# A feed-forward down projection with the block product as the outermost loop, and its weight sums made earlier

## Chip, cores and metric

The kernel runs on one core of a Trainium2 chip. The metric is device time in microseconds (us) of that core, from the first to the last instruction, lower being better. Engines are named as in the profile: PE is TensorE (matmuls), PEld its weight loads, DVE is VectorE, ACT is ScalarE, POOL is GpSimd, SP is SyncE, which here only issues transfers.

## What is computed

One layer of an encoder with D = 1024 channels, L = 2048 positions and a feed-forward width of 4096, all in float32. Cut to what matters here:

```python
h = h + mixed @ w_out                                    # Hyena and mLSTM groups
h = h + cross_attention(rms_norm(h), rms_norm(mem), ...) # 4 heads, 256 memory tokens
h = h + square(relu(rms_norm(h) @ ff_w1)) @ ff_w2        # (2048,1024)@(1024,4096), (2048,4096)@(4096,1024)
return rms_norm(h, final_norm_g)
```

The change concerns the last line of the layer: the second product, here called the down phase (`ff_w2`, W2), and the places in attention and in the first product (the up phase, `ff_w1`) beside which sums of W2 blocks are made.

## The kernel before

**Stages.** The Hyena and mLSTM parts fill the first 1640 us or so, woven into the first chunks of `attention`. `attention` goes through four chunks of 512 positions; in each it makes the output projection (eight column tiles `ct`), the attention scores and values, and the attention output (eight more column tiles). Then `ffn` runs the up phase and the down phase.

**Order.** The tile framework gives every engine its own queue in an order planned from estimated costs: an instruction is put as early as its inputs and its buffers allow, earlier lines first among those that are ready. On the chip each queue then runs in that order, and an instruction that waits holds up those behind it on its engine. Buffers come from rings: a tag with `bufs=4` has four buffers, given out in program order; the next user of a buffer waits until all users of the one before are done. A pool that is opened after another has closed may use its memory.

**Precision.** Every float32 operand is split into a high and a low half (`halves`: ScalarE casts the high half, another engine subtracts it to get the low one), and every product is three matmuls (`mm3`): high x high, high x low, low x high.

**Seven products instead of eight.** Both feed-forward matrix products use the Winograd form of Strassen's scheme: of a 2 x 2 x 2 block product only seven block products are made, of sums of blocks; sums of the seven give the four result blocks. The products are numbered 1 to 7. For the up phase the positions' blocks (x) are summed by `sums_x`, on POOL: four blocks are loaded, four sums made and stored in the scratch tensor `xs`; the sums of W1's blocks are made on POOL in `load_w1` and `ffn_w1`. The four sums of the activated blocks (c11, c12, c21, c22, tag `q`, seven buffers) are made on POOL at product 3 of each group (`t`, four buffers) and stored in the scratch tensor `hc`.

**Where sums of x are made.** `attention` pops one entry of the list `sums` at every odd column tile: 20 empty ones, then four `sums_x` for the first half of the positions (tag `sm`, four buffers). `ffn` makes the other four at product 4 of groups 3, 5, 7 and 9 of the first half (`tp` = 0), in the same four `t` buffers as the sums of c.

**The up phase** goes through 16 groups `g` of 256 hidden channels for each half `tp` of the positions, and in each through the seven products (`ORDER_UP`): 224 steps of 12 matmuls.

**The down phase** sums over 32 blocks of 128 hidden channels, which are 16 pairs. The pairs are cut into four quarters `o` of four. The loop is `prods = [(o, i) for o in range(4) for i in ORDER_DOWN]`: for each quarter the seven products, for each product both position halves `tp`, and for each of these four steps `k`, each of 12 matmuls into four banks; again 224 steps.
- `load_w` loads three blocks of W2 per pair (`w`, in the pool `wring` that is also used for W1 and is open to the end), `sums_w` and `fetch_a` make their sums, on DVE for the first quarter and on POOL for the others, and `fetch_a` splits the operand into `ah`, `al` (four buffers each). The split is by DVE for the first six products and by POOL after that.
- `fetch_b` loads an activation block three steps ahead and splits it into `bh`, `bl` (six buffers each). Every block that is split at once passes through the ring `wr` (six buffers).
- After every four steps the four banks go to a tile `acc[i, tp]`: ScalarE copies 24 of them, DVE adds the other 200 to what is there. In the last quarter the seven `acc` tiles of each half are added to each other, on DVE and POOL.
- `residual` loads 32 blocks of h2 and scales them on POOL into `acc` tiles, in steps 4 to 35.
- `turned` transposes result blocks on TensorE, `finish` normalises and stores them.

Of the kernel before, what the change touches and what calls it, by code (L numbers as in the profile page):

```python
# [133 lines left out]
class Prog:  # L134
# [1165 lines left out]

    def attention(self, es):
# [24 lines left out]
        sums = [None] * 20 + list(range(4))  # L1326
# [39 lines left out]
        for c in range(4):  # L1366
# [19 lines left out]
            for ct in range(8):  # L1386
                yield 5.2
                if ct % 2 == 0:
                    w = next(wst)
                else:  # L1390
                    k = sums.pop(0) if sums else None
                    if k is not None:
                        self.sums_x(A, k, "sm")
# [91 lines left out]
            for ct in range(8):  # L1485
                yield 5.2
                if ct % 2 == 0:
                    w = next(wst) if ct else w
                else:
                    k = sums.pop(0) if sums else None  # L1490
                    if k is not None:
                        self.sums_x(A, k, "sm")
# [37 lines left out]
    def halves(self, src, tags, bufs, eng):  # L1530
        hi, lo = (self.R.tile([128, 512], F32R, tag=n, name=n, bufs=bufs) for n in tags)
        self.nc.scalar.copy(hi, src)  # L1532
        eng.tensor_tensor(lo, src, hi.bitcast(F32), ALU.subtract)  # L1533
        return hi, lo

    def ffn_open(self, es):
        self.R = es.enter_context(self.tc.tile_pool(name="ring", bufs=1, side="right"))
        self.xt = {}
        self.W, self.WD = {}, {}
# [67 lines left out]
    def ffn(self):  # L1607
# [5 lines left out]
        self.C = self.ctx.enter_context(tc.tile_pool(name="wring", bufs=1))  # L1613
        prods = [(o, i) for o in range(4) for i in self.ORDER_DOWN]
        down = [(n, tp, k) for n in range(len(prods)) for tp in range(2) for k in range(4)]
        aq, bq = {}, {}

        def fetch_a(n, k):
            o, i = prods[n]
            w = self.blocks_of(2, 4 * o + k)  # L1620
            eng = nc.vector if n < 6 else nc.gpsimd
            if i in (6, 7, 5):
                if i == 6:
                    eng.tensor_tensor(self.WD[k, 0], self.WD[k, 2], self.WD[k, 0], ALU.subtract)
                src = self.WD[k, {6: 0, 7: 1, 5: 2}[i]]
            elif i == 1:
                src = self.WD[k, 0]
            else:
                src = self.raw(w[i == 4][1])
                if i == 3:  # L1630
                    eng.tensor_tensor(src, src, self.WD[k, 0], ALU.subtract)
            aq[n, k] = self.halves(src, ("ah", "al"), 4, eng)

        def load_w(o, k):
            w = self.blocks_of(2, 4 * o + k)
            for j, src in enumerate((w[0][0], w[1][0], w[1][1])):
                t = self.WD[k, j] = self.wtile()
                nc.sync.dma_start(out=t, in_=src)

        def sums_w(k, op=nc.gpsimd.tensor_tensor):  # L1640
            op(self.WD[k, 2], self.WD[k, 1], self.WD[k, 2], ALU.add)
            op(self.WD[k, 1], self.WD[k, 0], self.WD[k, 1], ALU.subtract)

        def fetch_b(s, eng=nc.vector):
            n, tp, k = down[s]
            o, i = prods[n]
            bq[s] = self.halves(self.raw(hc[tp, i - 1, 4 * o + k]), ("bh", "bl"), 6, eng)

        with tc.tile_pool(name="up", bufs=1) as U:
# [23 lines left out]
            for n, (tp, g, i) in enumerate(steps):  # L1673
# [7 lines left out]
                if n + 9 >= len(steps) and n + 5 < len(steps):  # L1681
                    load_w(0, n + 9 - len(steps))
# [4 lines left out]
                if i == 4 and xsum and g % 2 and 2 < g < 13:  # L1687
                    self.sums_x(U, xsum.pop(0), "t")
# [34 lines left out]
        with tc.tile_pool(name="down", bufs=1) as B:  # L1723
            acc, ms = {}, []
# [6 lines left out]
            for i in (1, 6, 7, 4, 5, 3, 2):  # L1731
                for tp in range(2):
                    acc[i, tp] = B.tile([128, 4, 512], F32, tag="acc", name="acc", bufs=14)
# [3 lines left out]
            def residual(i, tp, k):  # L1737
# [222 lines left out]
```

## Time and profile before

| | |
|---|---|
| Median of three runs | 3217.77 us (3217.51 to 3219.89) |
| The profiled execution's own time | 3216.99 us |
| Its span, first to last instruction | 3215.3 us |
| Mean granted TensorE clock | 0.981 |
| Busy share of PE, DVE, ACT, POOL | 95%, 63%, 47%, 37% |
| Moved by DMA | 617.87 MB, 192 GB/s on average |

How to read the profile: every row of a timeline has a start and a duration in us, the engine (with a q for a transfer that its queue issues), the line of the kernel, the operation, the tiles it writes and reads, and in brackets how long the engine had stood idle and what ended that. Rows of groups have the count, the busy time, the mean duration in ns, and the idle time before them. Most DMAs of the stages treated here are of 256 KB. Matmuls overlap, so it is the distance of their starts that counts, not their durations.

### The profile page before, as it was taken

To read this page: it belongs to the slowest core of one execution; us is meant where nothing else is said; L and a number is where in the kernel's file an instruction comes from. 1 tells how busy PE (TensorE), PEld (TensorE's weight loads), DVE (VectorE), ACT (ScalarE), POOL (GpSimd) and SP (SyncE) were. 2 spreads that over 40 slices of the span, in tenths; PEclk is the share of its full clock that TensorE was granted. 3 is DMA by queue.
4 is the path that set the end of the run, shared out by engine and by line. 5 is a ranking of instruction groups with operands and counts; after the bars stand their busy time and mean duration, and the time that the engine had idled before them with its cause. 6 is when DMAs were issued, how large, how long until landed. Compare 5 with 4: busy or idle time off the path is not lost.

```text
span 3215.3 us, 43642 instructions
## 1 busy us (share of the span) xinstructions
PE 3047.5 (95%) x14473; PEld 2394.2 (74%) x14473; DVE 2036.0 (63%) x3439; ACT 1500.1 (47%) x2873; POOL 1182.7 (37%) x818
## 2 busy tenths in 40 slices
PE   6999999999999976999999998999999999999998
PEld 4655566876668765878887886888788878888876
DVE  7775366345865755667775547556645676556595
ACT  5533366434764343454444445455555443333335
POOL 0122012100121334224151217776756483434483
PEclk9999999999999997999999999999999999999999
DMA  5564776686687989657484537665644474444434
GB/s 189 191 206 162 247 201 202 178 274 185 180 235 209 295 281 280 195 174 246 141 276 141 182 111 243 215 198 179 201 152 153 157 246 154 144 129 150 125 92 167
DMA packets 453817, 617.87 MB, mean 192 GB/s; under 512 B 39630, under 2 KB 251726, under 8 KB 452568
## 3 DMA queue, kind: packets, MB, share of 16 engines
q1 hardware_dynamic: 415412, 556.57, 55.2%
q10 hardware_dynamic: 38180, 58.51, 5.5%
q8 instruction: 115, 1.88, 0.2%
q14 instruction: 110, 0.90, 0.1%
HBM read 416.73 MB, written 198.21 MB: 191 GB/s over the span
## 4 chain that ended last, share of the span: by engine, by line
PE 71%; DMA 13%; DVE 8%; issue 3%; ACT 3%; POOL 1%; SPq 1%; ACTq 0%; DVEq 0%; POOLq 0%
PE mm L339 15%; PE mm L341 15%; PE mm L340 15%; PE hy L341 5%; PE hy L339 5%; PE hy L340 5%; PE hy L176 2%; DMA rw<-rows 2%; PE hy L875 1%; PE mm L844 1%; PE hy L917 1%; DVE wl L344 1%; DMA xt<-in_x_t_dram 1%; DVE bl L1533 1%; DMA va<-vd 1%
## 5 line engine op out<-in xcount | busy, mean ns | idle before, releaser
L344 DVE TENSOR_TENSOR wl<-wn,wh 128x512 fp32r<-128x512 f32 (+1 forms) x364 | 289.0, 829 | 125.5 <-ACT wh L344 124.9
L1533 DVE TENSOR_TENSOR bl<-wr,bh 128x512 fp32r<-128x512 f32 x213 | 241.1, 1138 | 126.8 <-ACT bh L1532 123.2
L1532 ACT CAST ah<-w 128x512 fp32r<-128x512 f32 x284 | 176.3, 622 | 300.1 <-PE hy L340 154.8
L344 ACT CAST wh<-wn 128x512 fp32r<-128x512 f32 (+1 forms) x364 | 207.9, 618 | 209.3 <-PE mm L341 47.8
L922 POOL TENSOR_TENSOR b<-b,a 128x512 f32<-128x512 f32 x64 | 87.7, 1370 | 581.4 <-ACT b L920 457.1
L339 PE MATMUL mm<-xh,wh 128*128 128x512 f32 x640 | 270.1, 423 | 4.5 <-ACT xh L499 2.3
L1533 DVE TENSOR_TENSOR al<-w,ah 128x512 fp32r<-128x512 f32 x236 | 222.0, 942 | 58.6 <-ACT ah L1532 58.6
L340 PE MATMUL mm<-xl,wh 128*128 128x512 f32 x640 | 256.7, 402 | 1.9 <-DVE xl L344 1.4
L341 PE MATMUL mm<-xh,wl 128*128 128x512 f32 x640 | 258.1, 404 | 0.0
L1532 ACT CAST bh<-wr 128x512 fp32r<-128x512 f32 x232 | 143.7, 621 | 240.0 <-PE mm L341 177.0
L341 PE MATMUL mm<-bh,al 128*128 128x512 f32 x576 | 225.4, 394 | 8.0 <-DVE al L1533 4.7
L339 PE MATMUL mm<-bh,ah 128*128 128x512 f32 x576 | 226.6, 393 | 0.1
L340 PE MATMUL mm<-bl,ah 128*128 128x512 f32 x576 | 225.8, 392 | 0.0
L339 PE MATMUL mm<-act,wh 128*128 128x512 f32 x512 | 199.0, 394 | 4.2 <-ACT act L344 2.7
L340 PE MATMUL mm<-act,wh 128*128 128x512 f32 x512 | 201.2, 394 | 0.0
L341 PE MATMUL mm<-act,wl 128*128 128x512 f32 x512 | 200.0, 392 | 0.3 <-DVE wl L344 0.3
L1382 POOL TENSOR_TENSOR ssum<-ssum,sq 128x512 f32<-128x512 f32 x56 | 81.1, 1448 | 287.7 <-ACT sq L1381 287.7
L339 PE MATMUL hy<-bh,ah 128*128 128x512 f32 x448 | 175.2, 391 | 0.0
L340 PE MATMUL hy<-bl,ah 128*128 128x512 f32 x448 | 174.6, 390 | 0.0
L341 PE MATMUL hy<-bh,al 128*128 128x512 f32 x448 | 174.4, 390 | 0.0
L339 PEld LDWEIGHTS mm<-xh,wh 128*128 128x128 f32 x640 | 121.1, 189 | 65.4 <-issue 29.5
L339 PE MATMUL hy<-xh,ah 128*128 128x512 f32 x384 | 152.2, 397 | 8.9 <-ACT ah L1532 8.2
(367 smaller groups left out, 8439.4 us busy)
## 6 DMA issues: line engine op xcount, KB each, us to landing
wr<-hc SPq DMA_DIRECT2D x224, 256.0 KB
w<-in_ff_w_dram SPq DMA_DIRECT2D x176, 256.0 KB
hc<-t SPq DMA_DIRECT2D x128, 256.0 KB
wn<-in_w_in_dram SPq DMA_DIRECT2D x100, 256.0 KB
hc<-q SPq DMA_DIRECT2D x96, 256.0 KB
fs<-a SPq DMA_DIRECT2D x32, 512.0 KB
a<-fs SPq DMA_DIRECT2D x64, 256.0 KB
a<-zs SPq DMA_DIRECT2D x64, 256.0 KB
```

The costliest lines, as they stand in the source:

```text
L176: b = self.nc.tensor.matmul(*products[-1], start=True, stop=True)
L339: mm(ps, lh, rh, start=start, stop=False)
L340: mm(ps, lh, rl, start=False, stop=False)
L341: mm(ps, ll, rh, start=False, stop=stop)
L344: both = (self.nc.scalar.copy(hi, src), self.nc.vector.tensor_tensor(lo, src, hi.bitcast(F32), ALU.subtract))
L844: nc.tensor.matmul(pp, dm[:, m], t[:, m], start=True, stop=True)
L875: nc.tensor.matmul(pg, em[:, m], y, start=True, stop=True)
L917: nc.tensor.matmul(pp, dm[:, m], t[:, m], start=True, stop=True)
L922: nc.gpsimd.tensor_tensor(xt, xt, hi[:, m], ALU.mult)
L1382: nc.gpsimd.tensor_tensor(ssum, ssum, sq, ALU.add)
L1532: self.nc.scalar.copy(hi, src)
L1533: eng.tensor_tensor(lo, src, hi.bitcast(F32), ALU.subtract)
```

## The change

The product becomes the outermost loop of the down phase: `prods = ORDER_DOWN`, and for each product and each half of the positions 16 steps `k`, one for each pair. The four banks collect all 16 steps, so they are emptied 14 times and not 56 times. All 16 split blocks of a product are kept for both halves: the first four in `ah`, `al`, the other twelve in `dh`, `dl` in the pool `down`. `fetch_a` loads a block, or a ready sum of blocks, and splits it on DVE; for the first product blocks 4 to 15 are fetched four steps ahead, for the others at the step of the second half in which the buffer is last used. All activation splits go to DVE.

The sums of W2's blocks are made by a new method `sums_w`, on POOL, and stored in a scratch tensor `ws`: for pairs 0 and 1 ahead of the four `sums_x` of attention, for pairs 2 to 11 behind them, and for pairs 12 to 15 in the up phase at product 4 of groups 4, 6, 8 and 10. `load_w` and the sums in the down phase go. The pool `wring` now closes with the up phase's pool.

The results of the products are put together as they come (`close`): DVE adds a bank to a running sum `T[role, tp]` (product 1 is copied by ScalarE), which makes 56 additions on DVE from banks and 8 copies. The residuals are loaded, scaled and added on POOL, one per step, when the sum they go to is there (`jobs`). Transposes are made at every third step.

```diff
+    def sums_w(self, pool, g, tag):
+        op = self.nc.gpsimd.tensor_tensor
+        ws = self.dram("ws", (4, 16, 128, 512))
+        w = self.blocks_of(2, g)
+        t11, t12, t21, t22 = self.four(pool, [w[m][k] for m in range(2) for k in range(2)], tag)
+        op(t22, t21, t22, ALU.add)
+        op(t21, t11, t21, ALU.subtract)
+        op(t11, t22, t11, ALU.subtract)
+        op(t12, t12, t11, ALU.subtract)
+        for j, t in enumerate((t22, t11, t21, t12)):
+            self.nc.sync.dma_start(out=ws[j, g], in_=t)
...
-        sums = [None] * 20 + list(range(4))
+        sums = [None] * 16 + [partial(self.sums_w, A, g, "sm") for g in range(2)]
+        sums += [partial(self.sums_x, A, i, "sm") for i in range(4)] + [partial(self.sums_w, A, g, "sm") for g in range(2, 12)]
...
-        self.C = self.ctx.enter_context(tc.tile_pool(name="wring", bufs=1))
-        prods = [(o, i) for o in range(4) for i in self.ORDER_DOWN]
-        down = [(n, tp, k) for n in range(len(prods)) for tp in range(2) for k in range(4)]
+        prods = self.ORDER_DOWN
+        down = [(n, tp, k) for n in range(len(prods)) for tp in range(2) for k in range(16)]
+        ws = self.dram("ws", (4, 16, 128, 512))
...
+        def fetch_a(n, k, *own):
+            w = self.blocks_of(2, k)
+            src = {1: w[0][0], 2: w[0][1], 4: w[1][1], 5: ws[0, k], 6: ws[1, k], 7: ws[2, k], 3: ws[3, k]}[prods[n]]
+            aq[n, k] = self.halves(self.raw(src), *(own or (("ah", "al"), 4, nc.vector)))
...
+        with tc.tile_pool(name="wring", bufs=1) as self.C, tc.tile_pool(name="up", bufs=1) as U:
...
-                if n + 9 >= len(steps) and n + 5 < len(steps):
-                    load_w(0, n + 9 - len(steps))
...
-                if i == 4 and xsum and g % 2 and 2 < g < 13:
-                    self.sums_x(U, xsum.pop(0), "t")
+                if i == 4 and tp == 0 and 2 < g < 11:
+                    if g % 2:
+                        self.sums_x(U, xsum.pop(0), "t")
+                    else:
+                        self.sums_w(U, 10 + g // 2, "t")
...
+            def residual(tp, n, h, role, k):
+                own = role == "c22"
+                v = T[role, tp][:, k] if own else B.tile([128, 512], F32, tag="rs", name="rs", bufs=3)
                 nc.sync.dma_start(out=v, in_=h2[2 * tp + n, :, 4 * h + k])
                 nc.gpsimd.tensor_tensor(v, v, ms[2 * tp + n], ALU.mult)
+                dst = v if own else T[role, tp][:, k]
+                nc.gpsimd.tensor_tensor(dst, v, T["u3", tp][:, k] if own else dst, ALU.add)
...
+            def close(i, tp, bank, last):
+                def plus(dst, role):
+                    for m in range(4):
+                        d = V.tensor_tensor(dst[:, m], bank[m], T[role, tp][:, m], ALU.add)
...
+                def late(n, h, role):
+                    jobs.extend(partial(residual, tp, n, h, role, k) for k in range(4))
+                if i == 1:
+                    T["m1", tp] = block()
+                    for m in range(4):
+                        nc.scalar.copy(T["m1", tp][:, m], bank[m])
+                elif i == 6:
+                    T["u2", tp] = block()
+                    plus(T["u2", tp], "m1")
+                    late(0, 0, "m1")
+                elif i == 7:
+                    T["u3", tp] = block()
+                    plus(T["u3", tp], "u2")
+                    T["c22", tp] = block()
+                    late(1, 1, "c22")
+                else:
+                    role = {5: "c22", 3: "u2", 2: "m1", 4: "u3"}[i]
+                    plus(T[role, tp], role)
+                    if i == 5:
+                        plus(T["u2", tp], "u2")
+                        late(1, 0, "u2")
+                        late(0, 1, "u3")
+                    outs.extend(turned(tp, i in (5, 3), i in (5, 4), role))
             for s, (n, tp, k) in enumerate(down):
...
+                if s + 3 < len(down):
+                    fetch_b(s + 3)
+                if n == 0 and tp == 0 and k < 12:
+                    fetch_a(0, k + 4, ("dh", "dl"), 12, V, B)
+                if jobs:
+                    jobs.pop(0)()
...
-                    self.mm3(bank[m], ah[:, msl], al[:, msl], bh, bl, k == 0, k == 3)
+                    self.mm3(bank[m], ah[:, msl], al[:, msl], bh, bl, k == 0, k == 15)
                 if tp and n + 1 < len(prods):
-                    fetch_a(n + 1, k)
+                    fetch_a(n + 1, k, *((("dh", "dl"), 12, V, B) if k > 3 else ()))
+                if outs and k % 3 == 2:
                     outs.pop(0)("mm" if tp else "hy")
...
+                if k == 15:
+                    close(prods[n], tp, bank, s + 1 == len(down))
```

123 lines of the change are left out of this document (24 added, 99 removed).

## The prediction

> **What bounds the kernel now.** First the page: the span and the engines' shares.
> ```profile
> span 3215.3 us, 43642 instructions
> PE 3047.5 (95%) x14473; PEld 2394.2 (74%) x14473; DVE 2036.0 (63%) x3439; ACT 1500.1 (47%) x2873; POOL 1182.7 (37%) x818
> ```
> TensorE works 95% of the span. So an edit pays only where TensorE stands still, and costs only where it makes TensorE stand still. The busy time by stage says where that is (columns: window, length, busy time of PE, PEld, DVE, ACT, POOL with counts, granted clock, DMA share, GB/s).
> ```profile
> 1800.00:1930.00 130.00, 130.00 (x595) 108.11 (x594) 65.59 (x122) 53.82 (x110) 19.58 (x14) 1.00 0.32 107
> 1975.00:2135.00 160.00, 160.00 (x708) 132.48 (x707) 100.29 (x125) 86.36 (x145) 128.15 (x87) 1.00 0.66 215
> 2295.00:2560.00 265.00, 265.00 (x1171) 219.44 (x1170) 145.35 (x203) 136.14 (x222) 156.56 (x110) 1.00 0.49 162
> 2560.00:2660.00 100.00, 95.19 (x406) 77.77 (x406) 81.92 (x72) 45.06 (x81) 77.01 (x48) 0.97 0.67 224
> 2660.00:3110.00 450.00, 449.75 (x1984) 372.17 (x1984) 290.51 (x347) 144.09 (x245) 205.66 (x143) 1.00 0.43 132
> 3110.00:3198.00 88.00, 84.26 (x417) 68.76 (x415) 63.32 (x112) 48.38 (x109) 50.58 (x37) 0.98 0.42 138
> ```
> Undisturbed, one matmul takes 265.00/1171 = 0.226 us, so a step of the down phase (12 matmuls) takes 2.72 us, before and after the change: 224 steps either way, with 128 transposes either way. The down phase (2560 to 3198) is therefore already near its floor. What it loses is in the list of TensorE's waits for that stretch, and in the clock behind the two long ones.
> ```profile
> PE mm L341 <- DVE al L1533: 4.7, 1, 4.7
> PE mm L341 <- POOL al L1533: 3.3, 2, 3.0
> ```
> ```profile
> 2648.44 0.39 PE L340 MATMUL mm<-bl,ah 128*128 128x512 f32 x1
> 2653.54 0.79 PE L341 MATMUL mm<-bh,al 128*128 128x512 f32 x1 [4.71 <-DVE al L1533]
> 2654.13 0.63 PE L339 MATMUL mm<-bh,ah 128*128 128x512 f32 x1
> 2654.56 0.63 PE L340 MATMUL mm<-bl,ah 128*128 128x512 f32 x1
> ```
> ```profile
> 2653.00:2662.00 9.00, 8.46 (x25) 6.76 (x26) 7.66 (x9) 4.47 (x9) 4.12 (x3) 0.64 0.81 256
> 3117.00:3122.00 5.00, 4.80 (x15) 3.58 (x16) 5.00 (x5) 1.14 (x2) 5.00 (x4) 0.67 0.30 101
> ```
> After the first wait matmuls start 0.43 us apart (2654.13, 2654.56): the clock is 0.64 for 9 us, another 9 x 0.36 = 3.2 us. After the second, 5 x 0.33 = 1.7 us. The whole loss is 4.7 + 3.3 + 3.2 + 1.7 = 12.9 us. That is all the down phase has to give.
>
> **Start of the down phase: +1.4 us.** Twelve of the 16 blocks of the first product get buffers (`dh`, `dl`) in the pool that is opened when the up phase's pool has closed. Block 4 is needed at step 4.
> ```profile
> 2560.72 0.39 PE L339 MATMUL mm<-bh,ah 128*128 128x512 f32 x1
> 2572.06 0.39 PE L339 MATMUL hy<-bh,ah 128*128 128x512 f32 x1
> ```
> ```profile
> 2559.98 0.69 DVE L1641 TENSOR_TENSOR w<-w 128x512 f32<-128x512 f32 x1 [2.91 <-DMA w<-in_ff_w_dram]
> 2565.51 0.68 DVE L1663 TENSOR_TENSOR q<-mm,u 128x512 f32<-128x512 f32 x1
> 2567.60 1.29 POOL L1713 TENSOR_TENSOR t<-q 128x512 f32<-128x512 f32 x1 [16.71 <-ACT q L1665]
> 2572.25 1.74 POOL L1716 TENSOR_TENSOR t<-q,t 128x512 f32<-128x512 f32 x1
> 2574.01 0.32 SPq L1654 DMA_DIRECT2D hc<-t  x1
> 2576.69 1.75 SPq L1729 DMA_DIRECT2D on<-msd  x4
> 2577.10 2.05 ACT L1815 COPY acc<-mm 128x512 f32<-128x512 f32 x4 [6.94 <-DMA hc<-t]
> ```
> ```profile
> L1532 ACT CAST ah<-w 128x512 fp32r<-128x512 f32 x62 | 38.7, 624 | 91.0 <-PE hy L340 91.0
> ```
> The new pool's first uses (`on`, `acc`) come at 2576.7 to 2577.1, when the last store of the up phase (2574.01) has landed. If that stays, block 4 is cast (0.62) and split (0.69) by 2578.0, TensorE stands 5.9 us at step 4 (2572.06), and loses about 3 us more at the lower clock: 9 us. ScalarE would stand in the same wait, with the casts of activations behind it; those of the next steps are as early as now. But the store's chain starts with the last `q`, at 2565.51, although its bank was full when the down phase's first matmul started, by 2561: VectorE was held up by a W2 sum that waited 2.91 us for its load, and by other sums, all of which the change removes. With `q` at 2561.0 the store lands 4.5 us earlier, at 2572.2, and block 4 is ready at 2573.5: a wait of 1.4 us. Ends 0 and 9; I take the 1.4, since every operation in the way is one of those removed.
>
> **Down phase, steady part: -12.9 us.** Both waits are for a split of a W2 block (`al`), which a product needs four steps after the last one used its buffer, and behind which stand sums of blocks, late loads and POOL.
> ```profile
> L1533 DVE TENSOR_TENSOR bl<-wr,bh 128x512 fp32r<-128x512 f32 x203 | 230.1, 1139 | 122.4 <-ACT bh L1532 118.8 <-DMA wr<-hc 1.4 <-DMA wr<-in_ff_w_dram 1.2
> L1817 DVE TENSOR_TENSOR acc<-mm,acc 128x512 f32<-128x512 f32 x100 | 64.5, 682 | 38.3 <-PE mm L341 38.3
> L1817 DVE TENSOR_TENSOR acc<-hy,acc 128x512 f32<-128x512 f32 x100 | 64.2, 679 | 16.5 <-PE hy L341 16.4
> L1533 POOL TENSOR_TENSOR al<-w,ah 128x512 fp32r<-128x512 f32 x48 | 67.5, 1409 | 119.7 <-ACT ah L1532 119.7
> L1533 POOL TENSOR_TENSOR al<-wr,ah 128x512 fp32r<-128x512 f32 x40 | 54.7, 1371 | 100.0 <-ACT ah L1532 100.0
> ```
> After the change a block is split 16 steps (43 us) ahead, not four (11 us); the sums come ready from memory. VectorE gives up about 200 - 56 = 144 evictions at 0.68 us (98 us) and the 24 closing adds, and takes 88 splits over from POOL and 15 of the activations. A half with weight splits then needs two splits a step: 2 x 0.69 = 1.4 us (as the sum at 2559.98, with POOL idle) or 2 x 1.14 = 2.3 us (the mean here), under 2.72 either way. POOL keeps 32 residuals of two operations of 1.4 to 1.7 us, about 100 us, and no split, so nothing of it feeds TensorE quickly. Loads: 224 activations and 112 blocks, against 224 and 96 now, at a similar rate (132 GB/s). Six activation splits (`bh`, six buffers) still run ahead, 13 us; four or eight evictions in a row (2.7 or 5.4 us) fit inside; they are what is late next, if anything. I take the whole 12.9 us as gained; the other end is one new wait like that at 2653, 7.9 us. The closing chain keeps its four adds, 16 transposes and output writes: 0.
>
> [...]
>
> **Attention: +2 us.** Twelve sums of W2 blocks (four loads, four POOL operations, four stores each) use the four `sm` buffers in order, two ahead of the four sums of x and ten behind them.
> ```profile
> PE hy L1463 <- POOL ssum L1382: 4.0, 1, 4.0
> ```
> ```profile
> 1681.22 1.29 POOL L1293 TENSOR_TENSOR sm<-sm 128x512 f32<-128x512 f32 x1 [0.94 <-issue]
> 1696.65 1.26 POOL L1293 TENSOR_TENSOR sm<-sm 128x512 f32<-128x512 f32 x1 [3.49 <-DMA sm<-hg]
> 1697.87 1.26 POOL L1382 TENSOR_TENSOR ssum<-ssum,sq 128x512 f32<-128x512 f32 x1
> ```
> The sums now run as soon as their input is there, one per 15.4 us (1681.22 to 1696.65). The last sum of x started at 1696.65, so the tenth behind it starts near 1851 and ends near 1860, ahead of the up phase (1930); POOL has room (19.58 of 130 us) and so have the DMAs (107 GB/s, and 2 MB per 15.4 us are 136 more). What they can cost is seen in the rows: POOL stood 3.49 us for a load with a square sum queued behind it, and TensorE waited 4.0 us for that (about 6 with the lower clock). The next such point is the end of chunk 3's first half, in the middle of the added sums. SP's queue gets 8 more transfers per sum, and a store that waits for POOL holds up weight loads behind it; those have four buffers ahead. Ends 0 and 6; I take 2, a third, since sums would fill about half of POOL's time there and only one that waits for its load does harm.
>
> **Up phase: +2 us.** Four sums of W2 go beside groups 4, 6, 8 and 10; groups 3, 5, 7 and 9 have their sums of x already. All share four `t` buffers with the block sums of c, in program order.
> ```profile
> 2041.07 1.29 POOL L1713 TENSOR_TENSOR t<-q 128x512 f32<-128x512 f32 x1 [2.71 <-ACT q L1665]
> 2054.12 1.50 POOL L1293 TENSOR_TENSOR t<-t 128x512 f32<-128x512 f32 x1 [4.16 <-DMA t<-hg]
> 2057.50 1.30 POOL L1294 TENSOR_TENSOR t<-t 128x512 f32<-128x512 f32 x1 [0.64 <-POOL w L1582]
> 2063.88 1.29 POOL L1713 TENSOR_TENSOR t<-q 128x512 f32<-128x512 f32 x1
> 2079.15 1.29 POOL L1713 TENSOR_TENSOR t<-q 128x512 f32<-128x512 f32 x1 [3.10 <-ACT q L1665]
> ```
> Two groups take 2079.15 - 2041.07 = 38.08 us, 19.04 each. With a sum of x between, c's sums start 22.8 us after those of the group before (2041.07 to 2063.88), and the next group makes good the 3.8 us. After the change no group does until the tenth. A sum of W2 starts with the last-loaded blocks (2057.50, not 2054.12), so 22.8 to 26.2 us; by estimate 24.5. The lag after eight groups: 4 x 3.8 + 4 x 5.5 = 37 us. `q` has seven buffers, four per group, so the fourth of the next group waits once c's sums are about 19 - 1.3 = 17 us late (less the time of two activations); eight PSUM banks let TensorE go on for up to another group, 19 us, if the rest is queued well. So TensorE loses between 0 and 37 - 17 = 20 us. I take 2, from the row that is nearest: with lags of 3.8 us TensorE was busy 160.00 of 160.00 us. POOL would be busy 128 + 16 x 1.4 = 151 of 160 us.
>
> **Sum.** -12.9 + 1.4 + 2 + 2 = -7.5 us. The profiled execution took 3216.99 us, which makes 3209.5; the median of the runs is 0.8 us higher: 3210 us. About 0.2%, 6.4 us, is what a measurement of this kernel can tell from no change: faster is below 3211.3, slower above 3224.2.
>
> **Rivals.** *The ring of `t` buffers becomes the bound in the up phase* (slower). For it: the 37 us of lag, the DMAs at 0.66 share with 8.4 MB more in 160 us, 32 more transfers in SP's queue among W1's loads, and W1's sums behind POOL's waits for loads (the 4.16 us). Against: banks and `q` buffers. Price 20 us in place of 2: 3228 us. It decides from a loss of 16 us. Chance 0.31.
>
> *The new pool opens as late as now* (no change): 9 us at step 4 instead of 1.4: 3218 us. For it: 2576.69. Against: the sums that are gone. Chance 0.15.
>
> *The change doesn't do what it says*: the down phase waits elsewhere, since loads and splits still pass through six `wr` buffers and one queue in order; one wait like 2653's, +7.9: 3218 us. Against: two waits in 224 steps, both at W2 blocks. Chance 0.12.
>
> [...]
>
> **Numbers.** The forecast has 0.42: faster. The two rivals at 3218 make no change 0.27, the first slower 0.31. Below, all added costs at nothing give 3217.8 - 12.9 = 3204.9, and 2 us for a shorter close; above, the first rival with 6 us in attention in place of 2 gives 3232, and a slower clock behind its waits a little more. The likeliest case alone: 3203 to 3211.
>
> **What would show it.** In the down phase no wait of TensorE over 1 us after step 4, and POOL near 100 us in place of 333. At step 4, about 1 us of wait for `dl` (9 with the clock: second rival). In 1975 to 2215 TensorE full; a wait there for `al`, `ah` or a bank, with c's sums more than 16 us late, is the first rival. I am wrong altogether if the up phase starts later than now (the tenth sum of W2 still open at 1930), or if TensorE's pitch differs from 0.226 us.

## The result and the profile after

The changed kernel takes 3269.2 us (median of five runs, 3266.1 to 3275.4), the kernel before 3219.4 on the same chip: 1.0158 times as long, 95% interval 1.0143 to 1.0172. The forecast was 3210 with a range to 3233, so it was wrong: the kernel became 50 us slower. First the page and the busy time by stage of the changed kernel, then the same four stages in the kernel before (window, length, busy time of PE, PEld, DVE, ACT, POOL with counts, granted clock, DMA share, GB/s).

```profile
span 3267.4 us, 43690 instructions
PE 3069.9 (94%) x14473; PEld 2401.6 (74%) x14473; DVE 1928.0 (59%) x3358; ACT 1491.9 (46%) x2857; POOL 1038.8 (32%) x723
...
1240.00:1297.00 57.00, 28.51 (x166) 26.49 (x165) 31.09 (x87) 16.25 (x67) 29.17 (x23) 0.65 0.87 282
1711.00:1830.00 119.00, 105.56 (x464) 85.45 (x465) 64.60 (x108) 46.01 (x97) 52.86 (x39) 0.93 0.79 265
2090.00:2250.00 160.00, 144.90 (x605) 117.31 (x605) 74.65 (x101) 67.72 (x117) 118.08 (x84) 0.95 0.65 215
2614.00:3252.00 638.00, 636.08 (x2813) 518.29 (x2812) 311.44 (x454) 229.09 (x414) 103.32 (x68) 1.00 0.51 161
```
```profile
1240.00:1285.00 45.00, 26.19 (x158) 24.85 (x159) 24.41 (x80) 15.30 (x64) 19.32 (x15) 0.66 0.83 256
1699.00:1798.00 99.00, 98.65 (x458) 81.28 (x459) 54.84 (x110) 46.22 (x98) 13.62 (x11) 0.98 0.55 183
2058.00:2218.00 160.00, 160.00 (x707) 132.48 (x707) 92.59 (x118) 84.81 (x139) 117.27 (x82) 1.00 0.56 183
2560.00:3198.00 638.00, 629.20 (x2804) 518.69 (x2803) 435.75 (x529) 237.53 (x434) 333.25 (x227) 0.99 0.46 147
```
The rows from 1240 on are the same work ahead of attention's chunk 0 in both kernels, and those from 1711 and 1699 the second half of chunk 2: both have become longer, and the DMA engines are fuller there. The rows from 2090 and 2058 lie 124 us into the up phase: there TensorE worked all of 160 us before and 145 after. In the down phase POOL is down from 333 to 103 us, as forecast, and TensorE is full, and yet the phase is no shorter. TensorE's waits in the changed kernel, for chunk 2's second half and chunk 3, the up phase and the down phase, and last the longest of the up phase in the kernel before:

```profile
PE hy L1356 <- DMA wn<-yh: 6.5, 2, 6.3
PE hy L1476 <- POOL ssum L1395: 4.0, 2, 3.7
PE hy L1356 <- DMA wn<-ym: 2.5, 1, 2.5
...
PE hy L339 <- ACT ah L1545: 21.0, 6, 4.7
PE hy L341 <- DVE al L1546: 4.5, 4, 2.7
...
PE mm L339 <- ACT dh L1545: 1.9, 1, 1.9
...
PE hy L339 <- ACT ah L1532: 8.2, 3, 4.6
```
The two waits of the down phase are gone; what is left is 1.9 us at step 4 (forecast 1.4). But 21.0 us of waits for `ah` stand in the up phase (8.2 in the kernel before) and 13.0 in attention's three rows (4.0 before). In the stretches that hold the long ones the granted clock was 0.93 and 0.95 (0.98 and 1.00 before).

The stages of every kernel below, from the first rows of their matmuls (start: first `act` matmul of chunk 0; attention: from there to the first `xh,ah` matmul of the up phase; up: from the first to the last of these; down: from there to the last `bh` row of L339; all us, each of one profiled execution; last the median, beside that of the kernel before measured with it):

| kernel | start | attention | up | down | median / before |
|---|---|---|---|---|---|
| before | 1285.3 | 648.5 | 626.2 | 636.5 | |
| after | 1296.7 | 669.2 | 648.3 | 636.2 | 3269.2 / 3219.4 |
| loop_alone | 1287.2 | 646.1 | 624.6 | 636.6 | 3217.6 / 3219.2 |
| sums_alone | 1301.8 | 669.4 | 650.3 | 636.2 | 3273.2 / 3219.2 |
| mid_sums | 1287.6 | 665.9 | 623.5 | 636.2 | 3232.8 / 3219.2 |
| dl_high | 1298.1 | 670.2 | 647.3 | 636.3 | 3269.5 / 3219.2 |
| loop_moved | 1292.3 | 649.0 | 624.5 | 625.1 | 3205.4 / 3224.5 |
| mid_staged | 1293.9 | 663.1 | 631.1 | 636.3 | 3237.2 / 3224.5 |
| staged | 1287.9 | 666.5 | 642.3 | 625.0 | 3240.9 / 3224.5 |
| mid_traffic | 1292.4 | 669.6 | 624.5 | 636.2 | 3239.4 / 3219.6 |
| late | 1290.0 | 654.5 | 636.6 | 626.6 | 3219.5 / 3219.6 |
| late2 | 1290.3 | 648.2 | 636.3 | 628.8 | 3217.3 / 3221.0 |

From before to after: +11.4 at the start, +20.7 in attention, +22.1 in the up phase, -0.3 in the down phase and -1.8 behind it make the 52.1 us by which the span grew. How far single executions scatter shows in kernels that have no sum of W2 in a stage: the start lies between 1285.3 and 1293.9, attention between 646.1 and 651.3, the up phase between 623.5 and 626.2 (without mid_staged, see below).

### The profile page after: what moved, and what is told of

The parts are those of the page before. It is cut to its first block, busy times and chain, and to the rows that moved or that the text cites. A ratio compares the mean times of both kernels' runs of the same rounds, so it can differ in the third digit from the quotient of the medians.

```text
span 3267.4 us, 43690 instructions
## 1 busy us (share of the span) xinstructions
PE 3069.9 (94%) x14473; PEld 2401.6 (74%) x14473; DVE 1928.0 (59%) x3358; ACT 1491.9 (46%) x2857; POOL 1038.8 (32%) x723
## 4 chain that ended last, share of the span: by engine, by line
PE 68%; DMA 15%; DVE 6%; issue 3%; POOL 3%; ACT 3%; SPq 1%; ACTq 0%; POOLq 0%; DVEq 0%
PE mm L339 14%; PE mm L340 14%; PE mm L341 14%; PE hy L341 5%; PE hy L339 5%; PE hy L340 5%; PE hy L176 3%; DMA hc<-t 2%; DVE wl L344 1%; PE hy L875 1%; PE mm L844 1%; PE hy L917 1%; DMA wn<-in_xa_wo_dram 1%; DMA rw<-rows 1%; DMA wn<-in_xa_wq_t_dram 1%
## 5 line engine op out<-in xcount | busy, mean ns | idle before, releaser
L1546 DVE TENSOR_TENSOR bl<-wr,bh 128x512 fp32r<-128x512 f32 x228 | 187.8, 826 | 203.7 <-ACT bh L1545 203.1
L1546 DVE TENSOR_TENSOR al<-w,ah 128x512 fp32r<-128x512 f32 x220 | 204.6, 931 | 121.8 <-ACT ah L1545 121.6
L339 PE MATMUL mm<-xh,wh 128*128 128x512 f32 x640 | 270.9, 424 | 5.4 <-ACT xh L499 3.2
L1545 ACT CAST ah<-w 128x512 fp32r<-128x512 f32 x220 | 135.3, 619 | 235.0 <-PE mm L340 103.8
L339 PE MATMUL mm<-act,wh 128*128 128x512 f32 x512 | 201.0, 398 | 9.0 <-ACT act L344 3.0
L339 PE MATMUL hy<-xh,ah 128*128 128x512 f32 x384 | 155.4, 405 | 21.8 <-ACT ah L1545 21.0
L339 PEld LDWEIGHTS mm<-xh,wh 128*128 128x128 f32 x640 | 121.6, 190 | 65.9 <-issue 29.2
L341 PE MATMUL hy<-xh,al 128*128 128x512 f32 x384 | 155.1, 404 | 4.5 <-DVE al L1546 4.5
L340 PEld LDWEIGHTS mm<-xl,wh 128*128 128x128 f32 x640 | 121.1, 189 | 50.9 <-issue 24.2
L340 PE MATMUL hy<-xl,ah 128*128 128x512 f32 x384 | 154.4, 402 | 1.8 <-POOL xl L1570 1.8
L339 PE MATMUL mm<-wh,xh 128*128 128x256 f32 (+1 forms) x512 | 152.3, 299 | 4.0 <-ACT st L202 3.3
L341 PEld LDWEIGHTS mm<-xh,wl 128*128 128x128 f32 x640 | 121.2, 189 | 41.3 <-issue 17.6
L339 PE MATMUL mm<-xh,ah 128*128 128x512 f32 x384 | 149.9, 390 | 0.0
L340 PE MATMUL mm<-xl,ah 128*128 128x512 f32 x384 | 149.8, 390 | 0.0
```

The source lines that it names most:

```text
L339: mm(ps, lh, rh, start=start, stop=False)
L340: mm(ps, lh, rl, start=False, stop=False)
L341: mm(ps, ll, rh, start=False, stop=stop)
```

## The experiments

**The loop alone, and the sums alone.** `loop_alone` has no `sums_w` call, and plain blocks where the loop reads sums:

```diff
-            src = {1: w[0][0], 2: w[0][1], 4: w[1][1], 5: ws[0, k], 6: ws[1, k], 7: ws[2, k], 3: ws[3, k]}[prods[n]]
+            src = {1: w[0][0], 2: w[0][1], 4: w[1][1], 5: w[0][0], 6: w[1][0], 7: w[1][1], 3: w[0][1]}[prods[n]]
```


> The new loop order without any sum of W2: products 5, 6, 7 and 3 read plain blocks of W2 of the same size in place of the sums, so the output leaves out the sums; loads, halves and matmuls of the down phase are the changed kernel's. Theory (the sums cost all of the loss, the loop alone is worth nothing because its matmuls are slower): the up phase starts at 1934 and lasts 627 as in the kernel before, the down phase lasts 636 as in the changed kernel, total 3217 to 3223, same. Rival 1 (the loop costs time by itself, through its later start or its larger set of halves): above 3235. Rival 2 (the slower matmuls come from the sums' traffic, not from the loop): the distance between two matmuls with dh or dl falls to 227 ns, the down phase to 625, total 3207 to 3211.

`sums_alone` is the kernel before with `sums_w` and its calls added, the result unused.

> The kernel before, with the sums of W2 made and stored at the changed kernel's places and used by nobody. Theory (the sums cost the loss, in three places that add up: 11 to 13 ahead of attention's first chunk, 19 to 21 in attention's chunk 2, 22 in the up phase): the up phase starts at 1966, lasts 648, the down phase lasts 636 as in the kernel before, total 3268 to 3276. Rival (the loss comes from both halves of the change together, since the loop's new buffers also shift the rest): under 3250.

Measured: loop_alone 0.9995 times the kernel before (0.9983 to 1.0007), sums_alone 1.0167 (1.0141 to 1.0193). The first `xh,ah` matmul of the up phase, in loop_alone and in sums_alone:

```profile
1933.31 0.50 PE L339 MATMUL hy<-xh,ah 128*128 128x512 f32 x1 [0.75 <-ACT xh L1568]
```
```profile
1971.16 0.50 PE L339 MATMUL hy<-xh,ah 128*128 128x512 f32 x1 [0.75 <-ACT xh L1569]
```
The halves of the change add up: the sums carry the whole loss, and the loop gains nothing, although its waits are gone. That leaves two questions: what ate the loop's gain, and what the sums cost where.

**What ate the gain: the place of `dh` and `dl`.** The changed kernel's matmuls were only slower with certain weights. Four rows of it: the first matmul of a half with `ah`, 48 later the first with `dh`, 144 later the first with `ah` of the next half, 48 later `dh` again.

```profile
2661.44 0.40 PE L339 MATMUL hy<-bh,ah 128*128 128x512 f32 x1
...
2672.38 0.40 PE L339 MATMUL hy<-bh,dh 128*128 128x512 f32 x1
...
2705.84 0.39 PE L339 MATMUL mm<-bh,ah 128*128 128x512 f32 x1
...
2716.74 0.40 PE L339 MATMUL mm<-bh,dh 128*128 128x512 f32 x1
```
With `ah` and `al`, 10.94/48 and 10.90/48 give 228 and 227 ns a matmul; with `dh` and `dl`, 33.46/144 is 232.4 ns, at a granted clock of 1.00 and with TensorE busy all of the time. The down phase has 2016 such matmuls: 2016 x 5.7 ns = 11.5 us, the gain. The first guess was the distance from `bh`: `dl` was put behind the ten `acc` blocks.

```diff
+            B.tile([128, 512], F32R, tag="dh", name="dh", bufs=12)
+            block()
```


> The changed kernel with the 12 buffers of dl placed behind the ten blocks of acc, at byte 125,024 to 149,600 of a partition, in place of 43,104 to 67,680; dh stays at 18,528. Nothing else differs. In the changed kernel a matmul with dh or dl comes 232.5 ns after the one before, with ah or al (byte 212,960 and up) 226.7 to 227. Theory 1 (the place of the stationary tile in the partition sets the pace, far from the moving tile bh at 188,384 being slow): the matmuls whose weight load falls on dl come down toward 227 to 230 ns, the rest stay at 232.5; the down phase is 2 to 4 shorter, total 3264 to 3268. Theory 2 (it isn't the place: the number of buffers, the pool or the program's length): all stay at 232 to 233, total 3269 within 2.

All rows stayed at 232.3 to 232.7 ns (232.4 in the changed kernel): theory 1 fell, and `dl` low or high in the partition, at byte 43,104 or 125,024, made no difference. But at both places the tiles begin 96 bytes beyond a multiple of 512, since the 128-byte tile `ss` is allocated ahead of them, while `ah` and `bh` begin 480 beyond one. `loop_moved` moves one line:

```diff
-            ss = B.tile([128, 4, 2, 4], F32, name="ss")
...
+            for n in ("dh", "dl"):
+                B.tile([128, 512], F32R, tag=n, name=n, bufs=12)
+            ss = B.tile([128, 4, 2, 4], F32, name="ss")
             V = nc.vector
```


> loop_alone (the new order, plain blocks in place of the sums, so the output leaves the sums out) with the small tile ss (128 bytes of a partition) placed behind dh and dl in place of ahead of them: dh then begins at byte 18,400 and dl at 42,976 of a partition, both 480 beyond a multiple of 512, as bh (188,384) and ah (212,960) do; in loop_alone, the changed kernel and dl_high they begin 96 beyond one. Theory (the place of the stationary tile modulo some power of two up to 512 sets the pace): every row with dh or dl falls from 232.5 ns to 226.7 to 228, the down phase from 636.5 to 624 to 627, total 3204 to 3210 beside 3219 before, faster. Rival (the pace comes from something else: the left end of the partition, the number of buffers): rows stay at 232 to 233, total 3216 to 3222.

The 144 matmuls from the first with `dh` to the next with `ah` in loop_moved:

```profile
2623.33 0.39 PE L339 MATMUL hy<-bh,dh 128*128 128x512 f32 x1
...
2655.97 0.39 PE L339 MATMUL mm<-bh,ah 128*128 128x512 f32 x1
```
32.64/144 = 226.7 ns. The down phase is 11.5 us shorter, and the kernel takes 0.9942 times that before (0.9927 to 0.9957). So the start decides here, 480 or 96 beyond a multiple of 512: the four matmuls `m` of a step take weights 512 bytes apart, and yet the 12 places in a step are alike, 226.4 to 227.6 ns in loop_moved and 231.1 to 233.7 in loop_alone. Three other places (by pads of 64, 80 or 96 words, or with `ss` between the two), each run once, were to show which tile counts.

> loop_alone (sums left out) with dh at byte 18,656 (224 beyond a multiple of 512) and dl at 43,552 (32 beyond one). A weight load runs beside the matmul ahead of it, so the row with bl,dh carries the loads of dl, the rows with bh,dl and bh,dh those of dh. Theory (modulo 256 decides: 480 and 224 are the same place, 32 and 96 are not): rows that carry loads of dh at 227 to 228 ns, the row that carries dl's at 231 or more. Rival 1 (modulo 512): all rows slow. Rival 2 (modulo 64 or 32: 480, 224 and 32 are the same place, but 96 is too): then loop_moved would show no gain either.

> loop_alone (sums left out) with dh at byte 18,400 (480 beyond a multiple of 512, as bh and ah) and dl at 43,104 (96 beyond one). In two_phases (dh 224, dl 32) the row bh,dl had 235.4 ns, bl,dh 229.1, bh,dh 228.5. Reading 1 (a matmul's own stationary tile sets its pace): row bh,dl at 231 to 234, the rows with dh at 226.5 to 228. Reading 2 (the load of the next weights beside it does): row bl,dh at 231 to 234, the two others at 226.5 to 228. Down phase 627 to 631 either way.

> loop_alone (sums left out) with dh at byte 18,528 (96 beyond a multiple of 512) and dl at 43,488 (480 beyond one): split_phase with the two exchanged. split_phase had 227.1 ns for the row bh,dh (weights of dh in use, dh loaded beside it), 232.4 for bl,dh (dh in use, dl loaded), 234.0 for bh,dl (dl in use, dh loaded). Reading 1 (the tile in use): bh,dl at 227, both rows of dh at 231 or more. Reading 2 (the tile loaded beside it): bl,dh at 227, the two others at 231 or more. Reading 3 (either is enough): all three at 231 or more.

| kernel | `dh`, `dl` beyond a multiple of 512 | row bh,dh | row bl,dh | row bh,dl | down |
|---|---|---|---|---|---|
| loop_moved | 480, 480 | 226.7 | 227.3 | 227.2 | 625.1 |
| loop_alone | 96, 96 | 232.7 | 232.6 | 232.5 | 636.6 |
| two_phases | 224, 32 | 228.5 | 229.1 | 235.4 | 633.1 |
| split_phase | 480, 96 | 227.1 | 232.4 | 234.0 | 633.3 |
| swap_phase | 96, 480 | 232.8 | 232.8 | 234.3 | 637.7 |

(Mean distance in ns to the next matmul's start.) split_phase fitted neither of its readings, and its down phase was over the 631 of both. At 96 against 480 either is enough, the tile in use or the tile being loaded beside it (reading 3 of swap_phase): the five rows of split_phase and swap_phase with a tile at 96 in one of these places have 232.4 to 234.3 ns, the one without 227.1. "In use" can't be told from "loaded beside the matmul before", since every matmul's weights are: in the changed kernel those of the matmul at 2830.33 were loaded from 2830.10 on, beside the matmul at 2830.09. two_phases fits none of its own theories: at 224 the pace is nearly the good one (228.5), and loading a tile at 32 costs little (229.1) while using it costs most (235.4). Why a place is slow stays open. Between loop_alone and loop_moved the start alone moved the down phase by 11.5 us.

**What the sums cost in attention.** `mid_sums` keeps the ten sums behind those of x and drops the first two and the four of the up phase.

> The changed kernel without the first two sums and without the four of the up phase; for those six blocks the products read plain blocks of W2, so the output leaves these sums out. The ten sums of attention's second half stay in their places. Theory (three separate costs): attention's chunk 0 begins as in the kernel before (first act matmul at 1285 in place of 1297), chunk 2 still takes 158 to 160 in place of 138, the up phase starts at 1953 to 1955 and lasts 627, total 3236 to 3241. Rival 1 (the loss of chunk 2 is a follow-up of the late start ahead of chunk 0): chunk 2 back to 138 to 142, total 3217 to 3224. Rival 2 (the up phase's 22 come from the store traffic or the late start and not from its own four sums): it still lasts over 640.

It took 1.0053 times as long (1.0038 to 1.0067): attention 17.4 us longer, the start and the up phase as before. The three costs are separate: each goes with its own sums. The second half of chunk 2, in loop_alone and in mid_sums, and POOL's longest wait in mid_sums:

```profile
1697.50:1796.80 99.30, 99.13 (x457) 82.13 (x458) 53.17 (x110) 46.59 (x98) 13.27 (x10) 0.97 0.53 179
```
```profile
1700.70:1815.70 115.00, 104.05 (x453) 83.39 (x454) 63.12 (x107) 45.08 (x95) 52.11 (x38) 0.92 0.79 266
...
POOL sm L1306 <- DMA sm<-in_ff_w_dram: 65.5, 10, 9.5
```
POOL stood 65.5 us for the sums' loads, so the queues looked guilty. `mid_staged` takes all sums of attention apart with generators, in eight buffers (the sums of x in the up phase too, in four of their own):

```diff
         t11, t12, t21, t22 = self.four(pool, [w[m][k] for m in range(2) for k in range(2)], tag, bufs)
+        yield
...
+        yield
         for j, t in enumerate((t22, t11, t21, t12)):
```


> mid_sums (ten sums of W2 and four of x in attention's second half, the other six left out) with each sum taken apart: its four loads are issued one slot ahead of its four operations, its four stores one step behind them, in 8 buffers in place of 4. In mid_sums POOL stood 65.5 us for the ten sums' loads between 1700 and 1865, SP's queue 50 us for POOL's operations and 24 us for finished stores. Theory (waits inside the queues, not bandwidth or POOL's own time, are the price): POOL's wait for loads under 15, chunk 2 from 162 down to 145 to 150, up phase's start at 1936 to 1942, total 3221 to 3227 in place of 3233. Rival (the extra 20 MB of traffic or POOL's work itself is the price): chunk 2 stays at 157 to 163, total 3230 to 3236.

The same half of chunk 2 in mid_staged, and POOL's wait:

```profile
1705.30:1819.80 114.50, 101.86 (x460) 83.00 (x459) 75.24 (x111) 46.65 (x96) 66.98 (x47) 0.96 0.89 308
...
POOL sm L1309 <- DMA sm<-in_ff_w_dram: 31.6, 7, 11.0
```
The kernel took 1.0044 times that before (1.0026 to 1.0062), about as long as mid_sums. The wait halved (it was to fall under 15) and the stretch did not move: 114.5 us. So half of the waits in the queues can go without any gain. The DMA engines are now at 0.89. `mid_traffic` keeps the loads and stores and drops the operations:

```diff
-        op(t22, t21, t22, ALU.add)
-        op(t21, t11, t21, ALU.subtract)
-        op(t11, t22, t11, ALU.subtract)
-        op(t12, t12, t11, ALU.subtract)
```


> mid_sums with the loads and the stores of the ten sums of W2 but without their forty operations on POOL: each loaded block is stored as it is, so the output leaves the sums out altogether. In mid_staged the waits in POOL's and SP's queues were halved and more, and the stretch between the statistics' two matmuls of chunk 2 (97 us in loop_alone, 115 in mid_sums) stayed at 114.5. Theory now (the DMA engines are full there: 14 of 40 slices at 9 between 1755 and 1840, 42.9 MB in 162 us in place of 22.6 in 142): that stretch stays at 108 to 116, total 3226 to 3234. Rival (POOL's operations are the price, by slowing VectorE beside them: wl took 958 ns in mid_sums and 698 in loop_alone): that stretch is back to 97 to 102, wl at 700, total 3214 to 3221.

```profile
1707.30:1824.70 117.40, 104.79 (x453) 85.81 (x454) 53.95 (x106) 45.28 (x95) 12.88 (x10) 0.90 0.90 312
...
SPq L1306 <- DMA sm<-in_ff_w_dram: 19.3, 22, 2.5
SPq L1284 <- DMA ws<-sm: 19.2, 23, 4.1
```
Without any operation the stretch is as long, 117.4 us, and the kernel takes 1.0066 times that before (1.0044 to 1.0088): POOL's work is not needed for the loss, the transfers alone are enough. But not with a free queue: between 1700 and 1825 SP stood 38.5 us for landings of the sums' own loads and stores (the last two rows), as long as in mid_sums (22.8 for POOL's operations and 16.6 for stores). Where it hurts is the middle of the stretch, where `wn<-yh`, attention's input for chunk 3, has to be loaded. Busy tenths of the DMA engines in 40 slices of 1.25 us with these loads' issues, in loop_alone (1735 to 1785), mid_traffic and the changed kernel (both 1740 to 1790):

```profile
DMA  0000349700799079900000005177999999999999
...
L1349 SPq DMA_DIRECT2D wn<-yh x4: 319/319/320, 1739.8 to 1742.3; - x4
```
```profile
DMA  9984996699998899996998999688999999999218
...
L1345 SPq DMA_DIRECT2D wn<-yh x4: 430/515/634, 1760.7 to 1763.2; - x4
```
```profile
DMA  7889976658958699966000996999958966799899
...
L1350 SPq DMA_DIRECT2D wn<-yh x4: 360/376/424, 1767.0 to 1770.3; - x4
```
In loop_alone the engines stand idle for a third of the 50 us and the loads go out 42 us into the stretch (1739.8 - 1697.5); with the traffic hardly a slice is free, and they go out at 53 us (1760.7 - 1707.3), too late for TensorE, which waits 5.3 us for them and 5.3 for `ym`. In the changed kernel they go out at 1767, after three empty slices: there not the engines but SP's queue held them. So both the queue and the traffic can delay these loads; in mid_staged, where SP stood only some 23 us for the sums, the engines are fuller (0.89, in mid_sums 0.79). What all the slow versions share is 20 MB more through SP's one queue; how much of the price is the queue's and how much the engines' stays open, since no run has one without the other. Over the stretch mid_traffic moved 312 GB/s at a DMA share of 0.90, loop_alone 179 at 0.53. POOL's operations do slow VectorE's splits: a split `wl` took 698 ns on average in loop_alone, 958 in mid_sums beside them, and 732 in mid_traffic beside the same traffic without them. But mid_traffic, nearly without that, lost as much:

```profile
L344 DVE TENSOR_TENSOR wl<-wn,wh 128x512 fp32r<-128x512 f32 x48 | 31.1, 698 | 14.1 <-ACT wh L344 14.0
```
```profile
L344 DVE TENSOR_TENSOR wl<-wn,wh 128x512 fp32r<-128x512 f32 x48 | 44.4, 958 | 24.9 <-ACT wh L344 24.5 <-DMA ws<-sm 0.3
```
```profile
L344 DVE TENSOR_TENSOR wl<-wn,wh 128x512 fp32r<-128x512 f32 x52 | 36.1, 732 | 29.3 <-ACT wh L344 29.3
```

**The start.** The first two sums need nothing but W2 and an open pool, so they run long before their place in the program. The changed kernel's loads for them, by the view of tile `sm`:

```profile
L1284 SPq DMA_DIRECT2D sm<-in_ff_w_dram x8: 332/542/1281, 1241.3 to 1273.8; - x8
```
They fall where the DMA engines stood at 0.83 already. The three kernels with these sums start chunk 0 at 1296.7 to 1301.8 (mean 1298.9), the twelve without at 1285.3 to 1293.9 (mean 1289.4): 9.5 us. Whether their traffic, their place in SP's queue or their eight operations on POOL cost it wasn't taken apart.

**The up phase, and other places.** In the changed kernel's up phase (2090 to 2240) POOL stood for the sums' loads too:

```profile
L1306 POOL TENSOR_TENSOR t<-t 128x512 f32<-128x512 f32 x3 | 3.9, 1286 | 20.1 <-DMA t<-in_ff_w_dram 20.1
```
It stood 6.7 us a sum, beside some 5.5 of work. What that does to TensorE:

```profile
2096.43 1.26 POOL L1293 TENSOR_TENSOR t<-t 128x512 f32<-128x512 f32 x1 [5.12 <-DMA t<-hg]
2097.65 1.26 POOL L1595 TENSOR_TENSOR w<-w 128x512 f32<-128x512 f32 x1
2098.95 0.62 ACT L1545 CAST ah<-w 128x512 fp32r<-128x512 f32 x1 [11.67 <-POOL w L1595]
2099.62 0.80 PE L339 MATMUL hy<-xh,ah 128*128 128x512 f32 x1 [3.52 <-ACT ah L1545]
```
A sum of W1 (`w`) stood on POOL behind a sum of x that waited for its load, ScalarE waited for `w`, and TensorE for the split. A sum of x waited like that before the change too (4.16 us at 2054.12), without harm; now POOL has a sum of x or W2 in every group up to the tenth, needs 23.0 us a group (before 22.8 and 15.3 in turn) and is behind. TensorE stands four times for this sum of W1 between 2090 and 2250 (3.5, 4.7, 4.5 and 1.8 us; three times a sum of x is ahead of it on POOL, the last time c's sums). With the slower clock behind them (0.64 from 2099.6 to 2108, behind the first) these waits cost 6.6, 7.1, 6.6 and 2.9 us against 226.8 ns a matmul: 23 us, as much as the phase lost.

`staged` is the whole change with all sums taken apart, none early, and `ss` moved.

> The whole change, with the sums taken apart in the same way in attention (12 sums of W2, behind the four of x, so that none can run ahead of attention's first chunk) and in the up phase (loads two steps of the group ahead of the operations, stores at the next group's start, in four buffers of their own), and ss placed behind dl as in loop_moved. Theory (three queue costs and the place of dh and dl explain the whole loss): chunk 0 begins at 1285 to 1288, attention loses 5 to 9 in place of 32, the up phase lasts 629 to 637 in place of 648, the down phase 624 to 627 in place of 636, total 3212 to 3224 (centre 3217), within 0.2% of the kernel before or just better. Rival (the sums' traffic and POOL time can't be hidden): total 3240 to 3258, gaining only the 11 of the down phase and the 12 ahead of chunk 0.

Measured 1.0049 (1.0037 to 1.0062), near its rival: the start and the down phase came as expected, the up phase gained only 6 of 22 us and attention 3 of 21, which is within the scatter. But the 6 us are a gain and a loss. In buffers of their own the first sums of x run ahead, to the start of the phase, where TensorE already waits for its operands (row of staged):

```profile
1963.60 1.27 POOL L1294 TENSOR_TENSOR s<-s 128x512 f32<-128x512 f32 x1
```
That is 9 us into the phase; in the changed kernel the first sum of x runs 78 us into it. The 300th matmul with a block of x comes 101.6 us into the phase in staged and 100.0 in mid_staged (whose up phase of 631.1 us has no sum of W2 at all), 91.9 in the changed kernel and 91.1 in mid_sums. From that matmul to the end it is 540.7 us in staged, 556.4 in the changed kernel, 532.4 in mid_sums: where they stand, the four sums taken apart cost 8 us in place of 24.

`late` puts the sums where both POOL and the DMA engines have room.

```diff
+                if tp and i == 1 and pipe:
+                    next(pipe.pop(), None)
+                if tp and i == 2 and 1 < g < 14:
+                    pipe.append(self.sums_w(U, 2 + g, "s"))
+                    next(pipe[0])
+                if tp and i == 4 and pipe:
+                    next(pipe[0])
```


> The whole change with the 16 sums of W2 in other places: four in the second half of attention's chunk 3 (their loads kept in program order, so that they don't run ahead), twelve in the up phase's second half, one beside each group, with four buffers of their own, loads two steps ahead of the operations and stores at the next group's start; ss behind dh and dl. Output the reference's. In loop_alone the DMA engines were busy 0.30 of the time between 1840 and 1930 and 0.47 between 2300 and 2500, against 0.48 to 0.85 at the changed kernel's places; POOL had 0.10 and 0.61. Theory (the price is DMA time and POOL time where they are short, not the sums as such): attention as in loop_alone plus 0 to 3, the up phase 627 to 636, the down phase 625, total 3207 to 3217, faster by 0.1 to 0.4%. Rival (each sum costs the up phase 4 to 5.5 us wherever it stands, since POOL is behind): up phase over 665, total over 3245.

Measured 1.0004 (0.9995 to 1.0013): the same work, 50 us cheaper (11 of them by the place of `dh` and `dl`), but no faster than before, where 0.1 to 0.4% had been expected. Twelve sums cost the up phase 12 us; the four in attention cost 3 to 8 (654.5, beside 646.1 to 651.3 without). `late2` takes attention's four and two more into the first product of the down phase:

```diff
+                if s in (2, 5, 8, 11, 14, 17):
+                    made = self.sums_w(B, 10 + s // 3, "s", 8)
+                    next(made)
```


> late with its four sums of attention's chunk 3 and two of its up-phase sums moved on: no sum of W2 in attention, ten beside groups of the up phase's second half (blocks 0 to 9), six in the down phase's first product (blocks 10 to 15, one every three steps from step 2 on, in eight buffers of their own), where POOL was busy 9.6 of 92 us in late and the DMA engines 0.74 and 0.55 of two stretches of 46. Output the reference's. Theory (a sum costs little where POOL and the DMA engines have room): attention as in loop_moved, the up phase 632 to 636 (late: 636.6 with twelve), the down phase 625 to 629, total 3211 to 3218, faster than before by 0.1 to 0.3%. Rival (the stores of the six sums or their loads delay the first product's halves): down phase over 632, total over 3220.

Measured 3217.3, 0.9989 times that before (0.998 to 0.9998), the one version with the reference's output that is faster than the kernel before, by 0.1%: clear of no change by little, and under the 0.2% that the prediction set as what can be told. Attention is free of cost; the up phase keeps its 12 us with ten sums as with twelve, which isn't explained, and the down phase takes 4. Since loop_moved stands at 3205, 16 sums cost some 12 to 16 us at the best places tried.

## Why the prediction was wrong

**Down phase, -12.9: the mechanism right, one step missing.** The waits went, POOL fell to 103 us, step 4 waited 1.9. With `ss` moved the loop is worth 0.58% by the medians, some 19 us, of which the stages show 13.3 (11.4 in the phase, 1.9 behind it). The step that failed is "a step of the down phase (12 matmuls) takes 2.72 us, before and after the change": it took 2.79 with `dh` and `dl`, which ate the gain. The prediction named that as what would make it wrong altogether, but gave it no chance.

**Attention, +2 (ends 0 and 6): measured +20.7.** The pace of the sums was nearly right (ten that started between 1725 and 1870, one per 16.1 us, forecast 15.4), the room was not. The step that failed is "and so have the DMAs", at 107 GB/s: that row is from 1800 to 1930, and seven of the ten sums fell into 1711 to 1830, where the kernel before already moves 183 GB/s (1699 to 1798). The price was taken from POOL's waits, and SP's queue was put at nothing ("those have four buffers ahead"). In the runs the loads that came too late were those of attention's input, behind the sums' transfers in SP's queue and on the DMA engines; mid_traffic showed that this costs as much without any of POOL's operations (1.0066 times the kernel before, mid_sums 1.0053). The shares of queue and engines stay open.

**The start: no term, measured about 9.5 (11.4 in the two profiles).** The two sums ahead of those of x were counted among attention's, though an instruction is put as early as its inputs and buffers allow.

**Up phase, +2 (ends 0 and 20): measured +22.1.** This is the first rival, near its price of 20. POOL's pace came as forecast: c's sums went from 2037.7 to 2221.7 in eight groups of 23.0 us, where 22.8 and 24.5 in turn were expected. The step that failed is the slack of 17 us in `q` and the banks, and the 2 us taken from a row with lags of 3.8. After the opening of the phase TensorE first stood at 2099.6, when three groups had taken 68.8 us in place of 59.1 before: a lag of 10, not 17. It waited for no bank but for the split of W1's blocks (`ah`, 21.0 us in the phase, 8.2 before), whose sums stand in POOL's queue too and have less slack. The rival names W1's sums among its reasons, yet takes its price from `q` and the banks; that this came so near is in part luck.

## What to carry to other kernels

Price added traffic in the very stretch where its queue order will put it, at slices of a few microseconds, and ask of every added operation how early it could run, not where it stands in the program. When a matmul loop gets new weight tiles, compare the distance of matmul starts with the old ones, and look at where the tiles begin: a 128-byte tile allocated ahead of them was worth 11.5 us here, 0.4%. Buffers of their own also let operations run ahead, to where they may cost more.

## What was not expected of the hardware

In these kernels the distance of two matmuls changed with the place where the stationary tiles begin in the partition: 226.7 to 227.3 ns in loop_moved, at 480 beyond a multiple of 512, where the moving tile begins too, 232.5 to 232.7 in loop_alone, at 96 beyond, up to 235.4 in two_phases, with `dl` at 32. With one tile at 96 and the other at 480, both the matmuls that use the tile at 96 and those beside which it is loaded were slow: 232.4 to 234.3 ns in split_phase and swap_phase, beside 227.1 for those with the tile at 480 in both places. Place alone, low or high in the partition (`dl` at byte 43,104 or 125,024), made no difference: 232.3 to 232.7 ns.
